# Four places for layer 0's modulation weights, VectorE's rows planned from step 2 on, and tiles of h at multiples of 64 bytes

## The chip, the cores and the metric

One NeuronCore of one Trainium2 chip runs the whole kernel. The metric is the device time of one execution in microseconds. The kernel before was run three times and once more with the hardware profiler; the profile is of that last execution.

## The reference

A network of four layers at width d = 2048 on 256 rows of x and 256 rows of a context. Layer 0 and layer 3 are Fourier layers, layer 1 is windowed attention, layer 2 a convolution layer. Each layer is of this form:

```
shift, scale, gate = split(silu(c) @ ada_w[l])   # "modulation": one column vector per 2048 features
h = rmsnorm(x) * (1 + scale) + shift             # for layer 0 for the context's rows too
z, u = halves of h @ w_in[l]
y = mixing of u with z                           # Fourier, attention or convolution, silu gates
x = x + gate * (y @ w_out[l])
```

Everything is fp32, and the results have to hold fp32's accuracy. The weights alone are over 400 MB read once from device memory.

## The kernel before

Every matrix product of fp32 values is made of three matmuls on split operands: a weight piece `raw` (512 KB or 256 KB) is loaded, ScalarE casts it to `whi` (line 180), VectorE takes `wlo = raw - whi` (line 181), and TensorE adds whi·hh, whi·hl and wlo·hh (lines 193 to 195). hh and hl are the high and low part of a tile of h (lines 457, 458, and 483 for the deferred form); one tile `hx` holds both.

A scheduler sets the order of every engine's instructions from the program's order, data dependences and priorities; `tc.high_priority(offset=...)` raises a block's priority. All weight loads go out on SyncE's queue (SP), in that order, and a load waits there for its place (a buffer of a pool's tag) to be free.

**Layer 0.** h is built while it is used: z = h @ w_in runs in nine `steps` over the 16 k-tiles (two of one k-tile, then seven of two), each step over four column groups (`cg`) of 512 columns, with eight results `accz`. Ahead of step j's h stand step j's modulation columns: `ada_tiles(k, n, j, ...)` computes them in four quarters q of 512 rows each. A quarter loads `aw` (lines 227 to 230, two DMAs) and issues four matmuls into four column groups of one bank `pa` (line 234); after the last, line 240 copies the bank out and line 242 brings it to columns with small matmuls against `sel`. The steps call the generator's next quarter between column groups. Quarters 0 and 1 of each step, and 2 and 3 of steps past the first, have their `aw` tiles in two places of a step's pool; the first step's quarters 2 and 3 lie in `wp`'s four places of tag "aw".

**Rows of later layers.** Beside the steps, `ada_v` computes modulation rows of layer 1 on (loads L330 into wp's "aw", VectorE multiply-adds L281 and L283), and `ada_a` the same on TensorE (L270, L234's kind of matmul). `plan(tiles, calls)` spreads k-tiles over the coming `step()` calls. Before, ada_v's calls start with step JZ = 8, the last; ada_a's also in the last, over four calls.

**colT** is the transposed collection of small parameter vectors: `rt` (L129) is one matmul behind four small loads on ScalarE's queue.

**out_proj** (layers 1 to 3, L1106, L1107) accumulates y @ w_out in banks `acco`; L1117 adds a bank times the gate to xT in two halves and so frees the bank; L418 collects the sum of squares for the next layer's norm, and L437 makes the row sums of it. Layer 3's first part uses a deferred norm (`Deferred`): h is built without the norm's factor (L483), with the shift as two more columns (256, 257) of the tile, and `leave` multiplies by the factor afterwards.

```
JZ = 8
ada_v.plan(TZ, max(1, 4 * (last + 1 - JZ) - 4))
ada_a.plan(A0Z, 4)
```

Of the kernel before, what the change touches and what calls it, by code (L numbers as in the profile page):

```python
# [11 lines left out]
F32 = mybir.dt.float32  # L12
F32R = mybir.dt.float32r
# [28 lines left out]
OWN = 1  # L42
BS = 3
BS3 = 0
JZ = 8
A0Z = 2
PB1 = 0
PB1O = 0
# [22 lines left out]
def dit_kernel(ctx: ExitStack, tc: tile.TileContext, x, c, ctxt, c_ctx, norm_g, ada_w, ada_b,  # L71
# [41 lines left out]
    csil0 = cp.tile([P, 4, 32], F32, name="csil0")  # L113
    nc.gpsimd.memset(csil0[:], 0.0)
    adabT = cp.tile([P, 192], F32, name="adabT")
    ngT = cp.tile([P, 64], F32, name="ngT")
    colT = cp.tile([P, 64], F32, name="colT")
# [63 lines left out]
                eng.tensor_sub(lv[:, c], iv[:, c], hv[:, c].bitcast(F32))  # L181
        return hi, lo

    def gemm_T(outs, piece, rhs, kts, pump=None, span=(0, KT), n=2):

        for i, kt in enumerate(kts):
            whi, wlo = piece(kt)
            for ci, (o, first) in enumerate(outs):
                for k in range(n):
                    hh, hl = rhs(kt + k)  # L190
                    a, b = whi[:, k, ci * P:(ci + 1) * P], wlo[:, k, ci * P:(ci + 1) * P]
                    st = first and kt + k == span[0]
                    mm(o, a, hh, start=st, stop=False, skip_group_check=True)  # L193
# [26 lines left out]
    def ada_tiles(k, n, j, pl, pa):  # L220

        w = 2 * P * n
        for q in range(4):
            if j == 0 and q > 1:
                aw = wp.tile([P, D // 2], F32, tag="aw", bufs=AWB, name=nm("aw"))[:].rearrange("p (k c) -> p k c", k=4)
            else:
                aw = pl.tile([P, 4, 512], F32, tag="aw", bufs=2, name=nm("aw"))
            for i in range(2):
                c0 = (1 - i) * D + P * k
                nc.sync.dma_start(aw[:, :, i * P * n:(i + 1) * P * n],  # L230
                                  ada_w[0, q * 512:(q + 1) * 512, c0:c0 + P * n].rearrange("(k p) c -> p k c", p=P))
            for g in range(4):
                cs = csil[:, 4 * q + g, :] if q else csil0[:, g, :]
                mm(pa[32 * g:32 * g + cs.shape[-1], :w], cs, aw[:, g, :w],  # L234
                   start=q == 0, stop=q == 3, skip_group_check=True)
            if q < 3:
                yield
        with tc.high_priority(offset=FH if j < FJ else 0):
            a = tmp()
            nc.scalar.copy(a[:, :w], pa[:, :w])  # L240
            for i in range(2 * n):
                mm(pa[:, 2 * i:2 * i + 2], a[:, i * P:(i + 1) * P], sel[:], start=True, stop=True)
            for i, c0 in enumerate((16 + k, k)):
                dst = modc[0][:, c0:c0 + n, :]
                nc.vector.tensor_add(dst, pa[:, 2 * n * i:2 * n * (i + 1)].rearrange("p (k o) -> p k o", o=2),
                                     adabT[:, c0:c0 + n].unsqueeze(2).to_broadcast([P, n, 2]))
                if i == 0:
                    nc.vector.scalar_tensor_tensor(dst, dst, 1.0, ngT[:, k:k + n].unsqueeze(2).to_broadcast([P, n, 2]),
                                                   op0=ALU.add, op1=ALU.mult)
        yield  # L250

    def ada_group(l, s, st):
# [209 lines left out]
    WX = 258  # L462

    def new_hx(kt, w=256):
        hx[kt] = hxp.tile([P, 2, w], F32R, tag=f"hx{kt}", name=nm("hx"))
        return hx[kt][:, 0, 0:256], hx[kt][:, 1, 0:256]

    class Deferred:

# [10 lines left out]
        def start(self, kt):  # L480
            hh, hl = new_hx(kt, WX)
            nc.scalar.activation(hh, xT[kt][:], AF.Identity, scale=scale(self.l, kt, 0))
            nc.vector.scalar_tensor_tensor(hl, xT[kt][:], scale(self.l, kt, 0), hh.bitcast(F32),  # L483
                                           op0=ALU.mult, op1=ALU.subtract)
            nc.scalar.copy(hx[kt][:, :, 256:WX], self.sh[:, kt, :].unsqueeze(2).to_broadcast([P, 2, WX - 256]))

        def rhs(self, kt):
            return hx[kt][:, 0, :], hx[kt][:, 1, :]

        def norm(self, st):  # L490

# [15 lines left out]

        def build(self, n):
            for kt in range(self.done, min(KT, self.done + n)):
                build_h(xT[kt][:], self.rs[:], self.l, kt, 0, hx[kt][:, 0, 0:256], hx[kt][:, 1, 0:256])  # L510
# [147 lines left out]
    hp = pool(l0, "h0")  # L658
    stp = ExitStack()
    aw0 = pool(stp, "aw0")  # L660
    psD = pool(l0, "psD0", PSUM)
    psa_box[0] = pool(l0, "psada0", PSUM)
    psA = pool(l0, "psA0", PSUM)
# [101 lines left out]
                     final_g.rearrange("(k p) -> k p", p=P)])  # L765
    h_start(1)
    last = len(steps) - 1
    ada_v.plan(TZ, max(1, 4 * (last + 1 - JZ) - 4))
    ada_a.plan(A0Z, 4)
    for j, (k0, n) in enumerate(steps):  # L770
        if j == 0:
            continue
# [1 line left out]
        for cg in range(4):  # L774
# [113 lines left out]

    def lhs1(kt, m):
        if m < 2:  # L890
            return hx[kt][:, 0, m * P:(m + 1) * P], hx[kt][:, 1, m * P:(m + 1) * P]
# [168 lines left out]
    yh = [None] * 8  # L1060

    def rhsx(kt):
        return hx[kt][:, 0, 0:256], hx[kt][:, 1, 0:256]

    for g in range(4):
        accs = [accA("accz") for _ in range(2)]
# [18 lines left out]
    def out_proj(l, piece, rhs, pmp, after, nxt=None):  # L1085
# [7 lines left out]
        for g, q in order:  # L1093
# [19 lines left out]
            if q == 3:  # L1113
                for ci, o in enumerate(banks.pop(g)):
                    kt = 2 * g + ci
                    for h in range(2):
                        nc.vector.scalar_tensor_tensor(xT[kt][:], o[:, 256 * h:256 * h + 256], gate(l, kt, 0), xT[kt][:],  # L1117
                                                       op0=ALU.mult, op1=ALU.add)
# [19 lines left out]
    def first_chunk(dfr, st, banks, piece, pump):  # L1138
# [10 lines left out]
            elif i > NORM[1]:  # L1149
                dfr.build(2)  # L1150

        gemm_T([(b[:, 0:WX], True) for b in banks], piece, dfr.rhs, range(0, KT, 2), pm)

    ada_v.until(1, 2)
    ada_v.plan(T1O, SV1)
# [163 lines left out]
    for cg in range(4):  # L1319
# [115 lines left out]
```

## Time and profile before

| | |
|---|---|
| median of 3 runs | 1928.76 us (1928.31 to 1929.91) |
| the profiled execution | 1928.43 us, of which its span is 1926.6 |
| TensorE busy | 1859.7 us (97%) |
| VectorE, ScalarE busy | 1447.1 us (75%), 901.2 us (47%) |
| moved by DMA | 433.64 MB, 225 GB/s |

A row of the stretches gives, for a part of the span, how long each engine was busy. The chain that ended last lists, for a time, which instruction or which load the rest waited for. "PE pa L234 <- DMA aw" reads: TensorE's matmul of line 234 waited for the load of a tile aw. A number such as 12.1 behind such a line is microseconds in all, the next the times, the last the longest. In a chain row the count (x8) includes weight loads.

### The profile page before, as it was taken

The page shows a single profiled execution, that of the slowest core. Times are in us where ns is not written, and L with a number is a line of the kernel's source. Part 1 is how long each engine was busy: PE and PEld are TensorE (multiplying, and loading weights), DVE is VectorE, ACT ScalarE, POOL GpSimd, SP SyncE. Part 2 cuts the span into 40 slices and gives each one's busy share as a digit, 9 for nine tenths or more (in the row PEclk, how much of TensorE's full clock was granted, in tenths as well). Part 3 has the DMA queues.
Part 4 walks back from the last instruction along what each step waited for, and adds up shares of the span by engine and source line. Part 5 has one row for each costly group of instructions (what it writes and reads, how often), then busy time and mean ns, then how long its engine had stood idle before and what let it go on. Part 6 is the DMA issues. An engine that isn't in the chain of part 4 may idle for free.

```text
span 1926.6 us, 30182 instructions
## 1 busy us (share of the span) xinstructions
PE 1859.7 (97%) x11143; PEld 1498.1 (78%) x11143; DVE 1447.1 (75%) x2733; ACT 901.2 (47%) x1642; POOL 234.3 (12%) x128
## 2 busy tenths in 40 slices
PE   6999999999999999999999999899999899999997
PEld 5566657777776687866689987899998788888886
DVE  4799954566653458987898696678899999997675
ACT  6333342233321225455556445444455657656553
POOL 0000000000000000000000002688893000000000
PEclk9999999999999999999999999999999999999999
DMA  8888877666677754741567696467776697785553
GB/s 258 273 299 290 304 248 262 204 225 220 237 244 265 263 193 146 242 163 55 186 197 261 205 321 231 148 219 235 230 246 198 212 305 244 246 282 175 164 175 131
DMA packets 247237, 433.64 MB, mean 225 GB/s; under 512 B 16214, under 2 KB 135734, under 8 KB 247090
## 3 DMA queue, kind: packets, MB, share of 16 engines
q1 hardware_dynamic: 245664, 430.00, 67.3%
q10 hardware_dynamic: 1426, 1.73, 0.3%
q8 instruction: 87, 1.43, 0.3%
q14 instruction: 60, 0.49, 0.1%
HBM read 429.56 MB, written 2.10 MB: 224 GB/s over the span
## 4 chain that ended last, share of the span: by engine, by line
PE 77%; DVE 11%; DMA 6%; ACT 3%; issue 3%; SPq 1%; POOL 0%; DVEq 0%; ACTq 0%; POOLq 0%
PE acco L1106 9%; PE accz L193 5%; PE accz L194 5%; PE accz L195 5%; PE acco L1107 4%; PE accu L213 4%; PE accu L215 4%; PE accu L214 4%; DVE wlo L181 3%; DMA aw<-in_ada_w_dram 3%; PE pa L270 3%; PE accg L193 3%; PE accg L195 3%; PE accg L194 3%; DVE pv L1226 3%
## 5 line engine op out<-in xcount | busy, mean ns | idle before, releaser
L180 ACT CAST whi<-raw 128x512 fp32r<-128x512 f32 (+1 forms) x761 | 539.9, 761 | 699.2 <-PE accz L194 135.1
L181 DVE TENSOR_TENSOR wlo<-raw,whi 128x512 fp32r<-128x512 f32 x674 | 491.0, 777 | 211.4 <-ACT whi L180 208.0
L181 POOL TENSOR_TENSOR wlo<-raw,whi 128x1024 fp32r<-128x1024 f32 x87 | 209.7, 2421 | 1230.5 <-ACT whi L180 1227.1
L283 DVE SCALAR_TENSOR_TENSOR adacc<-aw,csil,adacc 128x1024 f32<-128x1024 f32 x188 | 245.5, 1312 | 76.6 <-DMA aw<-in_ada_w_dram 76.2
L1106 PE MATMUL acco<-yh,whi 128*128 128x512 f32 x768 | 272.8, 399 | 3.2 <-DVE xT L1117 3.2
L195 PE MATMUL accz<-hx,wlo 128*128 128x256 f32 (+1 forms) x768 | 218.3, 285 | 5.9 <-DVE wlo L181 5.8
L1107 PE MATMUL acco<-yh,wlo 128*128 128x256 f32 x768 | 216.1, 282 | 3.8 <-DVE wlo L181 3.8
L193 PE MATMUL accz<-hx,whi 128*128 128x256 f32 (+1 forms) x768 | 217.7, 284 | 0.0
L194 PE MATMUL accz<-hx,whi 128*128 128x256 f32 (+1 forms) x768 | 217.2, 283 | 0.0
L1226 DVE SCALAR_TENSOR_TENSOR pv<-gp,dwT,pv 128x256 f32<-128x256 f32 x480 | 191.1, 482 | 20.7 <-ACT pv L1220 20.1
L1106 PEld LDWEIGHTS acco<-yh,whi 128*128 128x128 f32 x768 | 145.4, 190 | 38.3 <-issue 3.8
L195 PEld LDWEIGHTS accz<-hx,wlo 128*128 128x128 f32 x768 | 145.6, 190 | 9.2 <-DVE wlo L181 8.0
L1107 PEld LDWEIGHTS acco<-yh,wlo 128*128 128x128 f32 x768 | 146.0, 190 | 5.6 <-DVE wlo L181 5.4
L195 PE MATMUL accg<-hx,wlo 128*128 128x256 f32 x512 | 145.1, 283 | 2.9 <-POOL wlo L181 2.9
L193 PE MATMUL accg<-hx,whi 128*128 128x256 f32 x512 | 146.1, 286 | 1.1 <-ACT hx L457 1.1
L194 PEld LDWEIGHTS accz<-hx,whi 128*128 128x128 f32 x768 | 146.1, 190 | 1.3 <-issue 0.8
L193 PEld LDWEIGHTS accz<-hx,whi 128*128 128x128 f32 x768 | 146.0, 190 | 1.4 <-issue 0.9
L194 PE MATMUL accg<-hx,whi 128*128 128x256 f32 x512 | 144.6, 283 | 0.0
L193 PE MATMUL acco<-yh,whi 128*128 128x512 f32 (+1 forms) x272 | 106.0, 390 | 0.0
L193 PEld LDWEIGHTS accg<-hx,whi 128*128 128x128 f32 x512 | 97.3, 190 | 8.5 <-issue 6.9
L195 PE MATMUL acco<-yh,wlo 128*128 128x512 f32 (+1 forms) x272 | 103.6, 381 | 0.0
L194 PE MATMUL acco<-yl,whi 128*128 128x512 f32 (+1 forms) x272 | 103.5, 380 | 0.0
(275 smaller groups left out, 3602.2 us busy)
## 6 DMA issues: line engine op xcount, KB each, us to landing
aw<-in_ada_w_dram SPq DMA_DIRECT2D x376, 512.0 KB, 5.5
raw<-in_four_w_in_dram SPq DMA_DIRECT2D x126, 512.0 KB, 4.5
raw<-in_attn_w_in_dram SPq DMA_DIRECT2D x72, 512.0 KB, 3.8
raw<-in_conv_w_in_dram SPq DMA_DIRECT2D x128, 256.0 KB, 2.9
raw<-in_four_w_out_dram SPq DMA_DIRECT2D x32, 512.0 KB, 6.3
raw<-in_attn_w_out_dram SPq DMA_DIRECT2D x64, 256.0 KB, 4.5
raw<-in_conv_w_in_dram SPq DMA_DIRECT2D x32, 512.0 KB, 4.1
raw<-in_conv_w_out_dram SPq DMA_DIRECT2D x64, 256.0 KB, 4.3
```

Source lines behind the costliest of these rows:

```text
L180: nc.scalar.copy(hv[:, c], iv[:, c])
L181: eng.tensor_sub(lv[:, c], iv[:, c], hv[:, c].bitcast(F32))
L193: mm(o, a, hh, start=st, stop=False, skip_group_check=True)
L194: mm(o, a, hl, start=False, stop=False, skip_group_check=True)
L195: mm(o, b, hh, start=False, stop=kt + k == span[1] - 1, skip_group_check=True)
L213: mm(acc[:], hh, whi[:, k, :], start=st, stop=False)
L214: mm(acc[:], hh, wlo[:, k, :], start=False, stop=False)
L215: mm(acc[:], hl, whi[:, k, :], start=False, stop=kt + k == KT - 1)
L283: ins = nc.vector.scalar_tensor_tensor(acc[:, cs], aw[i][:], cc, acc[:, cs], op0=ALU.mult, op1=ALU.add)
L1106: mm(o[:], whi[:, k, cs], rhs(kt), start=kt == 0, stop=False, skip_group_check=True)
L1107: mm(o[:, :256], wlo[:, k, cs], rhs(kt)[:, :256], start=False, stop=kt == KT - 1, skip_group_check=True)
L1226: nc.vector.scalar_tensor_tensor(pv[:, :256], gt[:, t:t + 256], dwT[:, kt, t:t + 1], pv[:, :256], op0=ALU.mult, op1=ALU.add)
```

## The change

It has five parts. Layer 0's quarters 2 and 3 of every step take their tiles from wp's four "aw" places: for a step of two k-tiles each quarter then is two half tiles (two places, four DMAs of 256 KB in place of two of 512 KB), for a step of one k-tile one. ada_v's calls start with step 2 (JZ = 2), 12 k-tiles over 26 calls; ada_a (JA = 8) runs in the last step over two calls. hx becomes a plain tile of 512 or 528 columns with hl at byte 1024 or 1088 (before, the deferred form's hl lay at 1032); the shift's low column stands beside its high one in hh alone, the hl matmul takes 256 columns (`narrow`), and `leave` adds the second column with one small instruction. The residual adds of layers 1 to 3 get priority RES = 200. csil0 moves to the pool of layer 0's start, so layer 1's rows make padded copies of silu(c) for their first four k-tiles too.

```
+JZ = 2
+JA = 8
+RES = 200
...
-                    mm(o, a, hl, start=False, stop=False, skip_group_check=True)
+                    mm(o[:, :narrow] if narrow else o, a, hl, start=False, stop=False, skip_group_check=True)
...
-            if j == 0 and q > 1:
-                aw = wp.tile([P, D // 2], F32, tag="aw", bufs=AWB, name=nm("aw"))[:].rearrange("p (k c) -> p k c", k=4)
+            if q > 1:
+                aws = [wp.tile([P, D // 2], F32, tag="aw", bufs=AWB, name=nm("aw"))[:]
+                       .rearrange("p (k c) -> p k c", k=4 // n) for _ in range(n)]
             else:
-                aw = pl.tile([P, 4, 512], F32, tag="aw", bufs=2, name=nm("aw"))
-            for i in range(2):
-                c0 = (1 - i) * D + P * k
-                nc.sync.dma_start(...)
+                aws = [pl.tile([P, 4, 512], F32, tag="aw", bufs=2, name=nm("aw"))[:]]
+            r = 4 // len(aws)
+            for h, aw in enumerate(aws):
+                for i in range(2):
+                    c0 = (1 - i) * D + P * k
+                    r0 = q * 512 + h * r * P
+                    nc.sync.dma_start(aw[:, :, i * P * n:(i + 1) * P * n],
+                                      ada_w[0, r0:r0 + r * P, c0:c0 + P * n].rearrange("(k p) c -> p k c", p=P))
...
-                if fp and kt < 4:
-                    cs = csil0[:, kt, :]
-                elif fp:
+                if fp:
...
-        hx[kt] = hxp.tile([P, 2, w], F32R, tag=f"hx{kt}", name=nm("hx"))
-        return hx[kt][:, 0, 0:256], hx[kt][:, 1, 0:256]
+        t = hxp.tile([P, 528 if w == WX else 512], F32R, tag=f"hx{kt}", name=nm("hx"))
+        hx[kt] = t[:, 0:w], t[:, 272:528] if w == WX else t[:, 256:512]
...
             nc.scalar.copy(col, bank[:, 256:257])
+            nc.vector.tensor_add(col, col, bank[:, 257:258])
...
-    ada_v.plan(TZ, max(1, 4 * (last + 1 - JZ) - 4))
-    ada_a.plan(A0Z, 4)
+    ada_v.plan(TZ, 4 * (last + 1 - JZ) - 2)
+    ada_a.plan(A0Z, 4 * (last + 1 - JA) - 2)
...
-            if j == last:
+            if j >= JA:
                 ada_a.step()
...
-                    for h in range(2):
-                        nc.vector.scalar_tensor_tensor(xT[kt][:], o[:, 256 * h:256 * h + 256], gate(l, kt, 0), xT[kt][:],
+                    with tc.high_priority(offset=RES):
+                        for h in range(2):
+                            nc.vector.scalar_tensor_tensor(xT[kt][:], o[:, 256 * h:256 * h + 256], gate(l, kt, 0),
...
+        gemm_T([(b[:, 0:WX], True) for b in banks], piece, dfr.rhs, range(0, KT, 2), pm, narrow=256)
```

The scheduler sets the order anew. Three places follow. A tile's number counts the tiles made up to it: aw_382 and aw_421 are step 1's quarters 0 and 1, aw_531 and aw_570 its quarters 2 and 3, aw_617 and the next ones step 2's; aw_2094 and aw_2096 are halves of a row of layer 1.

SP's queue behind the context's loads, before:

```order
L230 DMA aw_382<-in_ada_w_dram 128x4x128 x2
L230 DMA aw_421<-in_ada_w_dram 128x4x128 x2
L156 DMA raw_628<-in_four_w_in_dram 128x512
L156 DMA raw_661<-in_four_w_in_dram 128x512
L230 DMA aw_531<-in_ada_w_dram 128x4x128 x2
L230 DMA aw_570<-in_ada_w_dram 128x4x128 x2
L330 DMA aw_2094<-in_ada_w_dram 128x1024
L230 DMA aw_617<-in_ada_w_dram 128x4x256 x2
L230 DMA aw_650<-in_ada_w_dram 128x4x256 x2
L156 DMA raw_694<-in_four_w_in_dram 128x512
L330 DMA aw_2096<-in_ada_w_dram 128x1024
```

and now:

```order
L235 DMA aw_382<-in_ada_w_dram 128x4x128 x2
L235 DMA aw_421<-in_ada_w_dram 128x4x128 x2
L235 DMA aw_531<-in_ada_w_dram 128x4x128 x2
L235 DMA aw_570<-in_ada_w_dram 128x4x128 x2
L235 DMA aw_617<-in_ada_w_dram 128x4x256 x2
L156 DMA raw_628<-in_four_w_in_dram 128x512
L235 DMA aw_650<-in_ada_w_dram 128x4x256 x2
L156 DMA raw_661<-in_four_w_in_dram 128x512
L235 DMA aw_683<-in_ada_w_dram 128x2x256 x2
L235 DMA aw_684<-in_ada_w_dram 128x2x256 x2
L156 DMA raw_697<-in_four_w_in_dram 128x512
```

Step 1's quarters 2 and 3 moved ahead of the raw weights, and the half rows of layer 1 are gone from here.

TensorE in step 8, the last of layer 0's z, where pa_2171 (now pa_2207) is layer 1's modulation bank and accz the results of z, before:

```order
L195 MATMUL accz_2195<-hh_351,wlo_2199 128x512
L270 MATMUL pa_2171<-aw_2228,csil 2x512 x2
L270 MATMUL pa_2171<-aw_2230,csil 2x512 x2
L270 MATMUL pa_2171<-aw_2236,csil 2x512 x2
L270 MATMUL pa_2171<-aw_2238,csil 2x512 x2
L193 MATMUL accz_2252<-hh_349,whi_2258 128x512
```

and now:

```order
L195 MATMUL accz_2248<-hl_350,whi_2253 128x512
L273 MATMUL pa_2207<-aw_2223,csil 2x512 x2
L196 MATMUL accz_2248<-hh_351,wlo_2254 128x512
L194 MATMUL accz_2249<-hh_349,whi_2253 128x512
L195 MATMUL accz_2249<-hl_350,whi_2253 128x512
L273 MATMUL pa_2207<-aw_2225,csil 2x512 x2
L196 MATMUL accz_2249<-hh_349,wlo_2254 128x512
```

Two groups of four that stood in a row are now pairs between z's matmuls.

VectorE in layer 2's out_proj, at the first residual adds; xT_88 and xT_89 became xT_86 and xT_87 by the count of tiles. Before:

```order
L283 SCALAR_TENSOR_TENSOR adacc_15025<-aw_15322,csil,adacc_15025 128x1024
L1117 SCALAR_TENSOR_TENSOR xT_88<-acco_14967,modc_86,xT_88 128x256
L181 TENSOR_TENSOR wlo_15245<-raw_15241,whi_15244 128x512 x2
L181 TENSOR_TENSOR wlo_15276<-raw_15272,whi_15275 128x512 x2
L1117 SCALAR_TENSOR_TENSOR xT_88<-acco_14967,modc_86,xT_88 128x256
L1117 SCALAR_TENSOR_TENSOR xT_89<-acco_14968,modc_86,xT_89 128x256
```

and now:

```order
L286 SCALAR_TENSOR_TENSOR adacc_15079<-aw_15376,csil,adacc_15079 128x1024
L1125 SCALAR_TENSOR_TENSOR xT_86<-acco_15021,modc_84,xT_86 128x256
L181 TENSOR_TENSOR wlo_15299<-raw_15295,whi_15298 128x512 x2
L181 TENSOR_TENSOR wlo_15330<-raw_15326,whi_15329 128x512 x2
L1125 SCALAR_TENSOR_TENSOR xT_87<-acco_15022,modc_84,xT_87 128x256
L1125 SCALAR_TENSOR_TENSOR xT_86<-acco_15021,modc_84,xT_86 128x256
```

The second bank's first add moved ahead of the first bank's second; the four wlo stay where they were.

More of the change, by code (lines that the diff above doesn't have):

```diff
@@ L44 @@
 BS3 = 0
-JZ = 8
+JZ = 2
+JA = 8
 A0Z = 2
@@ L112, in dit_kernel @@
     csil = cp.tile([P, KT, 2], F32, name="csil")
-    csil0 = cp.tile([P, 4, 32], F32, name="csil0")
-    nc.gpsimd.memset(csil0[:], 0.0)
     adabT = cp.tile([P, 192], F32, name="adabT")
@@ L182, in w_piece, with gemm_T @@
         return hi, lo
-    def gemm_T(outs, piece, rhs, kts, pump=None, span=(0, KT), n=2):
+    def gemm_T(outs, piece, rhs, kts, pump=None, span=(0, KT), n=2, narrow=None):
         for i, kt in enumerate(kts):
@@ L223, in ada_tiles @@
         for q in range(4):
-            if j == 0 and q > 1:
-                aw = wp.tile([P, D // 2], F32, tag="aw", bufs=AWB, name=nm("aw"))[:].rearrange("p (k c) -> p k c", k=4)
-            else:
-                aw = pl.tile([P, 4, 512], F32, tag="aw", bufs=2, name=nm("aw"))
-            for i in range(2):
-                c0 = (1 - i) * D + P * k
-                nc.sync.dma_start(aw[:, :, i * P * n:(i + 1) * P * n],
-                                  ada_w[0, q * 512:(q + 1) * 512, c0:c0 + P * n].rearrange("(k p) c -> p k c", p=P))
+            if q > 1:
+                aws = [wp.tile([P, D // 2], F32, tag="aw", bufs=AWB, name=nm("aw"))[:]
+                       .rearrange("p (k c) -> p k c", k=4 // n) for _ in range(n)]
+            else:
+                aws = [pl.tile([P, 4, 512], F32, tag="aw", bufs=2, name=nm("aw"))[:]]
[6 more added lines that the diff above has]
+                                      ada_w[0, r0:r0 + r * P, c0:c0 + P * n].rearrange("(k p) c -> p k c", p=P))
             for g in range(4):
                 cs = csil[:, 4 * q + g, :] if q else csil0[:, g, :]
-                mm(pa[32 * g:32 * g + cs.shape[-1], :w], cs, aw[:, g, :w],
+                mm(pa[32 * g:32 * g + cs.shape[-1], :w], cs, aws[g // r][:, g % r, :w],
                    start=q == 0, stop=q == 3, skip_group_check=True)
@@ L484, in start @@
                                            op0=ALU.mult, op1=ALU.subtract)
-            nc.scalar.copy(hx[kt][:, :, 256:WX], self.sh[:, kt, :].unsqueeze(2).to_broadcast([P, 2, WX - 256]))
+            nc.scalar.copy(hx[kt][0][:, 256:WX], self.sh[:, kt, :])
         def rhs(self, kt):
-            return hx[kt][:, 0, :], hx[kt][:, 1, :]
+            return hx[kt]
         def norm(self, st):
@@ L509, in build @@
             for kt in range(self.done, min(KT, self.done + n)):
-                build_h(xT[kt][:], self.rs[:], self.l, kt, 0, hx[kt][:, 0, 0:256], hx[kt][:, 1, 0:256])
+                build_h(xT[kt][:], self.rs[:], self.l, kt, 0, hx[kt][0][:, 0:256], hx[kt][1][:, 0:256])
             self.done = min(KT, self.done + n)
@@ L660, in dit_kernel @@
     aw0 = pool(stp, "aw0")
+    csil0 = aw0.tile([P, 4, 32], F32, name="csil0")
+    nc.gpsimd.memset(csil0[:], 0.0)
     psD = pool(l0, "psD0", PSUM)
@@ L890, in lhs1 @@
         if m < 2:
-            return hx[kt][:, 0, m * P:(m + 1) * P], hx[kt][:, 1, m * P:(m + 1) * P]
+            return hx[kt][0][:, m * P:(m + 1) * P], hx[kt][1][:, m * P:(m + 1) * P]
         t = hc[kt // 2]
@@ L1062, in rhsx @@
     def rhsx(kt):
-        return hx[kt][:, 0, 0:256], hx[kt][:, 1, 0:256]
+        return hx[kt][0][:, 0:256], hx[kt][1][:, 0:256]
     for g in range(4):
@@ L1115, in out_proj @@
                     kt = 2 * g + ci
-                    for h in range(2):
-                        nc.vector.scalar_tensor_tensor(xT[kt][:], o[:, 256 * h:256 * h + 256], gate(l, kt, 0), xT[kt][:],
-                                                       op0=ALU.mult, op1=ALU.add)
+                    with tc.high_priority(offset=RES):
+                        for h in range(2):
+                            nc.vector.scalar_tensor_tensor(xT[kt][:], o[:, 256 * h:256 * h + 256], gate(l, kt, 0),
+                                                           xT[kt][:], op0=ALU.mult, op1=ALU.add)
                     if dfr:
@@ L1150, in pm @@
                 dfr.build(2)
-        gemm_T([(b[:, 0:WX], True) for b in banks], piece, dfr.rhs, range(0, KT, 2), pm)
+        gemm_T([(b[:, 0:WX], True) for b in banks], piece, dfr.rhs, range(0, KT, 2), pm, narrow=256)
     ada_v.until(1, 2)
@@ L1335, in dit_kernel @@
         gemm_N(accs, lambda kt: w_piece(w_rows(wi, kt, cg * 512)),
-               lambda kt, m: (hx[kt][:, 0, m * P:(m + 1) * P], hx[kt][:, 1, m * P:(m + 1) * P]),
+               lambda kt, m: (hx[kt][0][:, m * P:(m + 1) * P], hx[kt][1][:, m * P:(m + 1) * P]),
                range(0, KT, 2), pump5u if cg == 0 else ada_v.step)
```

1 line of the change is left out of this document (added).

## The prediction

> **What bounds the kernel now.** I read the page's first block, then the busy time of each engine by stretches, then the chain that ended last where TensorE idles. The page's head:
>
> ```profile
> span 1926.6 us, 30182 instructions
> PE 1859.7 (97%) x11143; PEld 1498.1 (78%) x11143; DVE 1447.1 (75%) x2733; ACT 901.2 (47%) x1642; POOL 234.3 (12%) x128
> ```
>
> TensorE (PE) is busy for all but 67 us. The stretches (us; busy time of PE, weight loads, VectorE, ScalarE, GpSimd; clock, DMA share, GB/s) tell where those lie:
>
> ```profile
> 0.00:80.00 80.00, 60.73 (x363) 40.78 (x363) 44.00 (x96) 43.32 (x87) 0.85 (x7) 0.96 0.82 259
> 80.00:240.00 160.00, 158.19 (x768) 106.66 (x768) 147.66 (x217) 60.35 (x72) 0.00 (x0) 1.00 0.87 297
> 240.00:280.00 40.00, 39.12 (x176) 22.25 (x174) 25.92 (x40) 21.30 (x33) 0.00 (x0) 1.00 0.67 230
> 1440.00:1560.00 120.00, 110.19 (x750) 101.04 (x749) 111.65 (x230) 70.91 (x151) 23.71 (x10) 0.97 0.68 222
> 1560.00:1720.00 160.00, 152.28 (x920) 132.42 (x919) 152.63 (x236) 100.59 (x168) 0.00 (x0) 0.98 0.81 269
> ```
>
> So 19 us can be won in the first 80 us; in layer 0's z steps (80 to 240) only 1.8; in layer 2's out_proj and the way into layer 3 some 17. Everywhere else an added matmul costs its time. The chain at the start (start, length, what), the stretch 30 to 35, SP's issues, and a small load of ScalarE's queue (KB, us to landing):
>
> ```profile
> 36.99 0.38 PE pxt L700 x2
> 37.47 4.26 DMA aw<-in_ada_w_dram
> 41.86 0.66 PE pa L234 x8
> 42.95 9.30 DMA aw<-in_ada_w_dram
> 52.38 1.02 PE pa L234 x2
> 53.60 0.66 PE accz L193 x2
> ```
>
> ```profile
> 30.00:35.00 5.00, 5.00 (x45) 4.67 (x44) 0.69 (x1) 4.72 (x12) 0.00 (x0) 0.91 0.03 10
> ```
>
> ```profile
> 21.24 2.56 SPq L230 DMA_DIRECT2D aw<-in_ada_w_dram  x4
> 35.38 2.59 SPq L230 DMA_DIRECT2D aw<-in_ada_w_dram  x4
> 38.02 0.50 SPq L330 DMA_DIRECT2D aw<-in_ada_w_dram  x1
> ```
>
> ```profile
> tmp<-in_conv_ln_g_dram ACTq DMA_DIRECT2D x1, 8.0 KB, 7.2
> 43.05 0.43 ACTq L126 DMA_DIRECT2D tmp<-in_conv_ln_g_dram  x1
> ```
>
> Step 1's quarters 2 and 3 have no place until PE has used quarters 0 and 1; they are issued at 35.38, after five microseconds in which the DMA engines moved 10 GB/s. All that follows lands late: PE waits to 41.86 and to 52.38, and z of step 1 starts at 53.60.
>
> **The change part by part.**
>
> *Start (A).* In the new order these four loads stand right behind those of 21.24, so they land in the empty stretch, and the half row of layer 1 (38.02) leaves this place: they and it, 1.5 MB by their shapes, no longer stand ahead of step 2's loads. PE then meets its data when its transposes end, at 37.4 in place of 41.86. Step 0's second half (48 matmuls of 128x256; 0.12 us each by the pair rows at the end of this part, 5.8 us) ends near 45. Between it and step 1 now stand the transposition of colT, which needs the four small loads, and one modulation group of 1 us. With no wait, step 1 starts at 46.0 (7.5 us won); if a small load is issued at 43.05 and takes 7.2 as before, at 50.3 + 1.3 = 51.6 (2.0 won). The small loads now share the queues with less traffic; I take 50.4, nearer the row: −3.1.
>
> The modulation matmuls of two steps (ns min, median, max), the chain in the first steps, and a step in steady state; the last row is the time from issue to landing of 12 loads, min, median, max:
>
> ```profile
> L234 PE MATMUL pa<-aw,csil x64: 591/592/617, 101.7 to 150.8; 128*2 128x512 f32 x48, 128*32 128x512 f32 x16
> 73.19 0.31 DVE hl L458
> 74.75 0.95 PE pa L234 x2
> 80.08 0.96 PE pa L234 x6
> 86.82 0.97 PE pa L234 x8
> 96.70:125.10 28.40, 28.09 (x138) 18.99 (x137) 26.48 (x39) 10.73 (x13) 0.00 (x0) 1.00 0.86 296
> 109.54 0.92 SPq L230 DMA_DIRECT2D aw<-in_ada_w_dram  x2
> 116.27 0.92 SPq L230 DMA_DIRECT2D aw<-in_ada_w_dram  x2
> DMA to landing us min/median/max: 5.0/5.5/6.3
> ```
>
> One modulation group, four matmuls side by side in four column groups, takes 0.97 (x8 counts its weight loads too); the one matmul at 74.75 takes 0.95 and its three others 0.96. So a group that the order cuts in two costs 0.95 more. Step 2's aw_650 was cut and is now whole: −1.0. Step 3's first tiles are pulled ahead of a wait of PE for hl (VectorE, to 73.5; the queue of wlo ahead of it is shorter with an earlier start): −1.0, from the some 2 us idle there (bounds 0 and −2), and the one more cut group of step 3 falls into the rest. Start together: **−5.1** (−10 to −2).
>
> By the Trainium skill (TensorE: Matmul & The Clock Gate, Part 3, the mechanism) matmuls in different column groups overlap, and a set lasts about as long as one of them. The trace has 0.592 for one and 0.97 for a set of four, so it agrees only in that the set is far under four times one. By that rule a cut would cost 0.59: B below would be +3.0 and the time 1929.0; I go by the chain's 0.95.
>
> *Cut groups after the start (B).* By the new order steps 7 and 8 have one cut group more each, and layer 1's modulation block on TensorE, whose eight k-tiles now run over the two first column groups of step 8's plan rather than over four, has 22 group times in place of 19. Rows from there:
>
> ```profile
> 262.13 1.03 PE pa L270 x4
> 277.68 0.97 PE pa L270 x8
> PE pa L270 <- DMA aw<-in_ada_w_dram: 0.5, 2, 0.3
> ```
>
> Half a group costs 1.03, a whole one 0.97: 2 × 0.96 + 3 × 1.03 = **+5.0**, all on PE, which is busy 39.12 of 40 us there. Bounds: +3 if two cuts stand where PE would wait for a load anyway, +5.
>
> *Quarter 3's place (C).* From step 3 on, quarters 2 and 3 share two of the four places while rows of layer 1 hold the others, as I read the allocations; so in steps 3 to 5 quarter 3's four loads are issued only when quarter 2's matmuls are done. Before, each quarter was issued when the quarter two ahead of it was done, so a load had two of the 6.73 us between 109.54 and 116.27. Now it has one less the group: 6.73 − 0.97 = 5.8 us, against 5.5 to land plus 0.92 for the two issues of the first half: 0.6 late, the second half up to 1.5. Halves of 256 KB may land sooner than the 5.0 of whole loads: 0 to 1.5 per step, three steps: 0 to 4.5, I take 0.5 per step, near the first half's row: **+1.5**. SP stands still meanwhile; behind it are the next raw weights, of which three are held, so PE does not see that.
>
> By the Trainium skill (DMA: Bandwidth & Descriptors, Bandwidth) loads should be batched to 1 MiB or more, which speaks against halving quarters 2 and 3. No row here prices a half load of this shape; were halves as slow as whole loads, C would be +4.5 and the sum 3 us more.
>
> *Rows over all steps, JZ (D).* The rows added per step look like 1 MB of load and its VectorE work, in steps where VectorE has 26.48 of 28.40. But the scheduler had already hoisted such rows: by both orders the bytes asked for ahead of each raw tile differ by at most 2 MB up to the first u piece and by none from the third on. Zero for that. Ahead of the first u piece the row halves stand 14 in a run now (7 MB, 24 us at the 296 GB/s above) where four stood between raw tiles: bounds 0 and +3, the slack of three raw tiles covers most: **+0.5**.
>
> *Residual adds in out_proj, RES (E).* Rows of layer 2, chain and waits:
>
> ```profile
> 1530.84 0.41 DVE xT L1117
> 1531.38 0.47 PE acco L1106
> 1531.85 0.12 PE acco L1107
> 1533.15 0.43 PE acco L1106
> 1536.32 0.23 PE acco L1106
> PE acco L1106 <- DVE xT L1117: 3.0, 1, 3.0
> PE pss L437 <- DVE ss L418: 2.9, 1, 2.9
> ```
>
> PE waits 3.0 us for the first residual add's bank, then runs at half pace (0.43 for 0.23) from 1533.15 to 1536.32, another 1.6; the way into layer 3 has 2.9, and the clock of 0.98 in its stretch of 160 us is 3 us of full pace. In the new order the four wlo of 128x512 still stand ahead, and one add of the second bank is put before the first bank's second: the first bank is free 0.41 later, **+0.4**. Bounds: −4.6 (stall and tail gone) and +2 (a longer tail).
>
> *Tiles, narrow matmuls, leave (F).* VectorE rows of 1600 to 1720, the first kind with an aligned tile, the second with the 2064-byte one:
>
> ```profile
> L458 DVE SCALAR_TENSOR_TENSOR hx<-tmp,modc,hx 128x256 fp32r<-128x256 f32 x16 | 6.9, 459 | 0.0
> L483 DVE SCALAR_TENSOR_TENSOR hx<-xT,modc,hx 128x256 fp32r<-128x256 f32 x4 | 1.8, 486 | 0.0
> ```
>
> At most 27 ns × 16 = 0.4 won; four small adds (one column each; estimated at 0.15, a third of the 256-column rows) stand in a stretch that VectorE fills (152.63 of 160): **+0.3** (−0.4 to +1). csil0's move and four more pads, small VectorE work ahead of a load that is awaited: 0.
>
> Sum: −5.1 + 5.0 + 1.5 + 0.5 + 0.4 + 0.3 = +2.6. The profiled execution took 1928.43, 0.33 under the median of the runs and inside their spread: 1931.0.
>
> **The rivals.** A change is told from none beyond 0.2%, 3.9 us.
> 1. *Slower, quarter 3's wait:* it takes 1.5 us in each of three steps or reaches the later steps. Sum 2.6 + 3.0 = 5.6, 1934.0; it decides from 0.95 us per step. For it: 5.5 + 1.84 for four issues against 5.8. Against: half the bytes per load.
> 2. *Slower, the small loads:* step 1's start still waits (start term −2): 5.7, 1934.1. For it: 7.2 us for 8 KB. Against: emptier queues.
> 3. *Faster, RES frees out_proj's banks* and PE stays at pace in both places: 2.6 without E's and F's 0.7, less 9: −7.1, 1921.3. For it: 4.6 us lost at the first and, by wait and clock, 4.4 and more at the second. Against: the wlo rows that stay ahead.
> 4. *Faster, start at 46.0*, with two cuts that stand in waits: 2.6 − 4.4 − 2 = −3.8, 1924.6. For it: the empty stretch of the DMA engines from 30 to 35. Against: colT.
> 5. *Nothing measurable:* cuts cost one lone matmul (0.59) each and start pays for them: 0.6, 1929.0.
>
> **How the numbers follow.** Forecast 0.34, rival 1 0.14, rival 2 0.14, rival 3 0.14, rival 4 0.12, rival 5 0.12. The likeliest's own range is 1927 to 1935; with one in ten left out on each side, 1921 to 1939. Faster 0.26, same 0.46, slower 0.28.
>
> **What would show it.** A: SP's eight modulation loads in a row before 30 us, accz of step 1 near 50. B: more pa groups, PE without new waits from 243 on, and u some 5 us later behind z's first step than now. C: waits of PE pa for aw near 0.5 us in steps 3 to 5, and SP waiting for PE there. E: the 3.0 us wait for xT still in layer 2. The prediction is wrong if the stretch 0 to 80 gives back over 8 us or nothing, or if the two late waits are gone.

## The result, and the profile after

The change makes the kernel slower: 1945.59 us (median of 4 runs, 1942.07 to 1949.18) against 1928.53 for the kernel before (1927.74 to 1929.91), a ratio of 1.0088 (95% interval 1.0074 to 1.0102), some 17 us. 1931.0 with a range of 1921 to 1939 was predicted.

The head of the page, and the stretches in which the two kernels can be compared by the clock of the span (same columns as before):

```profile
span 1947.1 us, 30248 instructions
PE 1871.5 (96%) x11143; PEld 1505.1 (77%) x11143; DVE 1447.6 (74%) x2745; ACT 901.0 (46%) x1642; POOL 234.5 (12%) x128
```

```profile
0.00:80.00 80.00, 64.96 (x384) 43.87 (x385) 46.18 (x98) 45.21 (x88) 0.84 (x7) 0.96 0.87 271
80.00:240.00 160.00, 152.93 (x692) 103.21 (x691) 132.25 (x198) 52.93 (x65) 0.00 (x0) 0.95 0.79 261
240.00:280.00 40.00, 37.70 (x169) 22.42 (x168) 29.91 (x47) 19.20 (x26) 0.00 (x0) 1.00 0.74 244
```

In the first 80 us TensorE is busy 4.2 us more than before. In the next 160 us, where it had idled 1.8 us, it now idles 7.1, the clock that it was granted is 0.95 in place of 1.00, and the DMA engines move less, 261 GB/s for 297. So most of the loss is in z's steps, and neither the DMA engines nor VectorE (132 for 148) are fuller than they were.

The steps can be measured by one instruction that each has once, ScalarE's copy of the next step's modulation bank at the step's end (L240, now L245). The first two rows are of the kernel before (step 2's end and step 7's), the others of the changed kernel (step 2's end to step 7's):

```profile
95.22 0.68 ACT L240 COPY tmp<-pa 128x512 f32<-128x512 f32 x1
237.30 0.65 ACT L240 COPY tmp<-pa 128x512 f32<-128x512 f32 x1
```

```profile
92.37 0.77 ACT L245 COPY tmp<-pa 128x512 f32<-128x512 f32 x1
125.98 0.71 ACT L245 COPY tmp<-pa 128x512 f32<-128x512 f32 x1
157.18 0.69 ACT L245 COPY tmp<-pa 128x512 f32<-128x512 f32 x1
188.83 0.70 ACT L245 COPY tmp<-pa 128x512 f32<-128x512 f32 x1
218.89 0.65 ACT L245 COPY tmp<-pa 128x512 f32<-128x512 f32 x1
248.99 0.64 ACT L245 COPY tmp<-pa 128x512 f32<-128x512 f32 x1
```

Before, five steps took 142.1 us, 28.4 each. Now step 2 ends 2.8 us earlier, but steps 3 to 7 take 33.6, 31.2, 31.7, 30.1 and 30.1, together 14.5 more: step 7 ends 11.7 late. The first row sum of layer 1 (L437, now L440) comes at 741.4 in place of 725.4, 16.0 late, so step 8 and u add 4.3.

What a long step waits for is in the chain of waits. The end of step 3:

```profile
115.57 1.19 DVE adacc L286
116.78 0.37 SPq L235
117.19 0.46 SPq L235
117.71 6.40 DMA raw<-in_four_w_in_dram
...
125.09 1.17 ACT whi L180
126.27 0.43 ACT tmp L245
126.74 1.17 PE pa L247 x8
127.92 0.64 PE accz L195
128.55 0.43 PE accz L196
...
131.34 0.23 PE accz L194
```

VectorE finishes with a half row of layer 1 (adacc); that frees its place, which a quarter's load (L235) has waited for at the head of SyncE's queue; only behind it can the next raw weights be issued, which land 6.4 us later. ScalarE casts them, and its copy of the bank stands behind the casts. TensorE stops for 2.2 us, and then its matmuls come every 0.43 us and not every 0.23 until 131. Step 4 ends by the same chain (a half row of VectorE until 148.7, then raw weights that land 5.6 us after their issue at 149.7). The waits of SyncE's queue from 60 to 250, first of the changed kernel, then of the kernel before (us in all, times, longest):

```profile
SPq L235 <- DVE adacc L286: 32.2, 9, 8.5
SPq L333 <- DVE adacc L286: 23.0, 5, 10.9
SPq L235 <- DVE adacc L284: 5.4, 2, 2.8
```

```profile
SPq L230 <- PE pa L234: 86.5, 24, 5.2
SPq L330 <- DVE adacc L283: 3.3, 2, 2.0
```

SyncE stood 3.3 us for VectorE's rows before and stands 60.6 now. The total is not what hurts: all waits that the profile lists for SyncE in these 190 us add up to 137 us before and 131 now. Before, the 86.5 us for a quarter's place left the raw weights in time.

### The profile page after: what moved, and what is told of

Read it like the earlier page. It is cut to its first block, busy times and chain, and to the rows that moved or that the text cites. A ratio compares the mean times of both kernels' runs of the same rounds, so it can differ in the third digit from the quotient of the medians.

```text
span 1947.1 us, 30248 instructions
## 1 busy us (share of the span) xinstructions
PE 1871.5 (96%) x11143; PEld 1505.1 (77%) x11143; DVE 1447.6 (74%) x2745; ACT 901.0 (46%) x1642; POOL 234.5 (12%) x128
## 4 chain that ended last, share of the span: by engine, by line
PE 77%; DVE 10%; DMA 8%; ACT 3%; issue 2%; SPq 0%; DVEq 0%; ACTq 0%
PE acco L1113 7%; PE accz L194 6%; PE accz L195 6%; PE accz L196 6%; PE accu L214 4%; DVE wlo L181 4%; PE accu L216 4%; PE accu L215 4%; PE acco L1114 3%; PE pa L273 3%; DMA aw<-in_ada_w_dram 3%; PE accg L194 3%; PE accg L196 3%; PE accg L195 3%; PE acco L194 3%; PE acco L195 3%
## 5 line engine op out<-in xcount | busy, mean ns | idle before, releaser
L194 PE MATMUL accz<-hx,whi 128*128 128x256 f32 (+1 forms) x768 | 218.0, 284 | 0.0
L195 PE MATMUL accz<-hx,whi 128*128 128x256 f32 x768 | 217.5, 283 | 0.0
L1234 DVE SCALAR_TENSOR_TENSOR pv<-gp,dwT,pv 128x256 f32<-128x256 f32 x480 | 191.1, 483 | 23.4 <-ACT pv L1228 20.5
L795 DVE TENSOR_TENSOR y<-accz,y 128x512 f32<-128x512 f32 x128 | 84.5, 687 | 30.8 <-PE accz L196 30.4
```

Of the source, the lines that this page charges most:

```text
L195: mm(o[:, :narrow] if narrow else o, a, hl, start=False, stop=False, skip_group_check=True)
L795: nc.vector.tensor_add(y, accs[ci][:], y)
L1234: nc.vector.scalar_tensor_tensor(pv[:, :256], gt[:, t:t + 256], dwT[:, kt, t:t + 1], pv[:, :256], op0=ALU.mult, op1=ALU.add)
```

## The experiments

Theory P at first: rows and quarters share places, so loads on SyncE's queue wait for VectorE. Its rivals: quarter 3's own missing place; 256 KB loads; the rows' work itself; the parts behind layer 0. The table has the ends of steps 2 and 7, the step times between, the first row sum of layer 1 (all from one profiled execution each), and the median and ratio of the runs.

| kernel | step 2 ends | steps 3 to 7 | step 7 ends | layer 1 | median, ratio to before |
|---|---|---|---|---|---|
| before | 95.2 | 28.5 28.4 28.3 28.4 28.4 | 237.3 | 725.4 | 1928.5 |
| changed | 92.4 | 33.6 31.2 31.7 30.1 30.1 | 249.0 | 741.4 | 1945.6, 1.0088 |
| rows_late | 92.6 | 28.5 28.4 28.5 28.4 28.5 | 234.8 | 758.0 | 1958.5, 1.0164 (1.0126 to 1.0202) |
| places_alone | 90.9 | 28.4 28.5 28.4 28.4 28.4 | 233.1 | 753.3 | 1959.9, 1.0163 (1.0141 to 1.0185) |
| rows_own_places | 95.2 | 30.2 30.2 30.1 28.4 28.5 | 242.6 | 729.7 | 1935.5, 1.0046 (1.0033 to 1.0058) |
| late_parts_alone | 94.0 | 28.5 28.4 28.5 28.4 28.5 | 236.2 | 724.6 | 1928.6, 1.0005 (0.9990 to 1.0020) |
| rows_on_gpsimd | 90.6 | 29.4 29.1 29.2 29.0 31.4 | 238.6 | 730.8 | 1932.8, 1.0025 (1.0012 to 1.0038) |
| rows_and_quarters_on_gpsimd | 91.9 | 29.1 29.1 29.3 29.0 30.1 | 238.6 | 730.2 | 1936.3, 1.0039 (1.0025 to 1.0052) |
| split_places | 93.9 | 28.8 28.5 29.1 28.4 31.1 | 239.7 | 734.8 | 1945.3, 1.0092 (1.0072 to 1.0111) |
| ada_a_old_plan | 92.0 | 32.3 33.1 30.0 30.1 30.2 | 247.7 | 735.7 | 1942.5, 1.0076 (1.0054 to 1.0098) |
| start_alone | 93.7 | 28.4 28.5 28.3 28.4 28.4 | 235.7 | 723.1 | 1926.2, 0.9993 (0.9981 to 1.0005) |
| places_to_step_3 | 92.4 | 28.5 29.4 28.3 28.4 28.4 | 235.4 | 722.1 | 1925.1, 0.9987 (0.9977 to 0.9997) |

What follows layer 1's start took between 1198.4 and 1208.2 us in these executions (before 1201.2, changed 1205.7); rows_own_places, which has the order of before there row for row, took 1205.9. So of the profiled execution's 20.5 us over before, the last 4.5 are within what one execution differs from another, and the mark at layer 1 is the better measure. The marks have their own spread: ada_a_old_plan has the changed kernel's order of instructions up to 265 us, and its steps 3 to 7 add up to 155.7 us where the changed kernel's have 156.6, with up to 2 us between single steps; rows_late and places_alone have one order up to 280 us, and their step 2 ends at 92.6 and 90.9.

**rows_late**

```
 # the changed kernel
-JZ = 2
+JZ = 8
-    ada_v.plan(TZ, 4 * (last + 1 - JZ) - 2)
+    ada_v.plan(TZ, max(1, 4 * (last + 1 - JZ) - 4))
```

> The changed kernel with ada_v's rows planned as before (JZ = 8, old formula); everything else of the change stays. Theory P (shared places: a modulation load waits on SP for VectorE to finish with a row that holds the place, and the raw weights queued behind it come too late): without rows in steps 2 to 7 no load waits for VectorE, the steps are back at 28.4 us in place of 30.1 to 33.6, and of the 15 us lost in steps 4 to 8 nearly all are won back; 1926 to 1932 in all. Rival Q (quarter 3 has one place less and PE waits for it): the places of quarters 2 and 3 are then free of rows, so four places serve both; this rival gives the same here, 1926 to 1932. Rival H (halves of 256 KB are slower to load): no change, 1940 to 1949. Rival L (the loss lies in the parts behind layer 0): no change.

**places_alone**

```
 # the kernel before, with the changed kernel's loads of quarters:
-            if j == 0 and q > 1:
-                aw = wp.tile([P, D // 2], F32, tag="aw", bufs=AWB, ...)
+            if q > 1:
+                aws = [wp.tile([P, D // 2], F32, tag="aw", bufs=AWB, ...) for _ in range(n)]
```

> The kernel before with the four places alone (ada_tiles of the change, the rows planned as before). Theory P: no rows hold the places during steps 2 to 7, steps at 28.4 us, the start earlier by 2.5 us: 1924 to 1930. Rival H: 256 KB halves are slow, 1940 and over. Rival Q: at most 1935.

Both have steps of 28.4 us, as theory P and rival Q had it, and both are far slower than the changed kernel, which no theory had (rival H's time for places_alone, 1940 and over, came, but not by slower steps). The steps first: with four places and no rows, quarter 3's own wait costs nothing, nor do halves of 256 KB, though SyncE waits long for it. Rivals Q and H fall. A rival that was not named falls as well, that TensorE's new order costs the time: up to 180 us the traces of places_alone and of the changed kernel have TensorE's and ScalarE's instructions in the same order, with steps of 28.4 in the one and of 31.2 to 33.6 in the other. What differs is VectorE's rows and SyncE's loads. PE's waits (60 to 330) and SyncE's (60 to 300) in places_alone, and its last step (step 8, to u's start):

```profile
PE accz L193 <- DVE y L792: 16.9, 4, 9.1
```

```profile
SPq L234 <- PE pa L238: 58.1, 17, 4.7
```

```profile
233.10:291.90 58.80, 39.84 (x146) 25.87 (x145) 51.53 (x64) 21.19 (x32) 0.00 (x0) 0.85 0.85 295
```

Step 8 takes 58.8 us; it was 41.3 before (237.3 to u's first matmul at 278.6). The kernel before has its rows in the program only from step 8 on too, but there the scheduler pulled them into the earlier steps, since wp's places were free; with the quarters in those places it cannot: the kernel before has issued 28 loads of half rows by 237 us, places_alone 6, the first at 225.7. So VectorE has 51.5 us of work in the last step (27.5 before), and PE waits for it to empty its banks (y). That is what the new plan of the rows repairs (step 8 takes 48.7 us in the changed kernel): it is the other half of the change, and without it the places cost 31 us. Step 8 has 17.5 of the 32.1 us that places_alone loses between step 7's end and layer 1; the rest comes in u and was not followed.

**rows_own_places**

```
 # the kernel before
-JZ = 8
+JZ = 2
-    ada_v.plan(TZ, max(1, 4 * (last + 1 - JZ) - 4))
+    ada_v.plan(TZ, 4 * (last + 1 - JZ) - 2)
```

> The kernel before with the rows' new plan alone (JZ = 2, 12 k-tiles over 26 calls): quarters keep their own two places, rows keep theirs. Theory P: rows and quarters share nothing, so SP waits for VectorE only with a row, as before; steps at 28.4 to 28.8 us, 1926 to 1932 in all. A rival W (it is the rows' work itself: 26.5 us of VectorE in a step of 28.4, or their loads): steps at 30 us and more, 1940 or over.

Three steps of 30.2, then 28.4. The time, 1935.5, lies between the two forecasts. It is no rival W: VectorE has 26.5 us in the slow steps as in the quick ones. The three slow steps are the three whose modulation group the order cuts in two, one each; the steps with four whole groups take 28.4. So this run prices a cut, with what comes with it: 1.7 to 1.8 us. TensorE's rows around one:

```profile
103.25 0.40 PE L195 MATMUL accz<-hh,wlo 128*128 128x512 f32 x1
104.06 0.73 PE L193 MATMUL accz<-hh,whi 128*128 128x512 f32 x2 [0.41 <-ACT hh L457]
...
105.42 1.02 PE L234 MATMUL pa<-aw,csil 128*2 128x512 f32 x2
106.37 0.50 PE L194 MATMUL accz<-hl,whi 128*128 128x512 f32 x1
106.70 0.39 PE L195 MATMUL accz<-hh,wlo 128*128 128x512 f32 x1
106.94 0.39 PE L194 MATMUL accz<-hl,whi 128*128 128x512 f32 x1
```

The one matmul holds TensorE from 105.42 to 106.37, the matmul after it takes 0.33 in place of 0.23, likewise the one ahead of it, and 0.41 more goes to a wait for hh, since these matmuls start before h is there.

**late_parts_alone**

```
 # the changed kernel, with before's loads of quarters, and
-JZ = 2
+JZ = 8
-    ada_v.plan(TZ, 4 * (last + 1 - JZ) - 2)
-    ada_a.plan(A0Z, 4 * (last + 1 - JA) - 2)
+    ada_v.plan(TZ, max(1, 4 * (last + 1 - JZ) - 4))
+    ada_a.plan(A0Z, 4)
```

> The changed kernel with layer 0's weights, rows and plans as before: what is left is hx's tiles with the narrow matmuls, the residual adds' priority 200, and csil0's move with four more pads. Theory P: within 3 us of before, 1926 to 1932 (the trace of the changed kernel has 1440 to 1720 within 2 us of before). Rival L: 1934 to 1945.

No change that can be measured: the tiles of h at multiples of 64 bytes, the narrow matmuls, the residual adds' priority and csil0's move together bring at most 2 us and cost at most 4, by the interval. Rival L falls.

Theory P had its place right but not its whole: it became theory T, in which SyncE's queue is what hurts, and cut groups a second cost.

**rows_on_gpsimd and rows_and_quarters_on_gpsimd**

```
 # the changed kernel
+    rowq = [nc.gpsimd]            # back to nc.sync behind z
...
-                nc.sync.dma_start(t[:], ada_w[l, ...])
+                rowq[0].dma_start(t[:], ada_w[l, ...])
 # and in the second of the two
-                    nc.sync.dma_start(aw[:, :, ...
+                    (nc.gpsimd if j > 1 and q > 1 else nc.sync).dma_start(aw[:, :, ...
```

> The changed kernel with the loads of layer 1's rows issued from GpSimd's queue instead of SyncE's while z of layer 0 runs; VectorE's and TensorE's work is the same, as are the places. Theory T (in steps 3 to 5 SyncE stands still before a load whose place a VectorE row still holds, so that the raw weights behind it are issued too late; a cut modulation group costs 1.2 to 1.8 us): only the quarters' own waits for such a place are left on SyncE's queue; the steps that had 33.6, 31.2 and 31.7 us fall to 28.4 to 30.5; step 6 and 7, whose cut groups are gone in this order, to 28.4; 1930 to 1940. Rival B (the places themselves: a quarter's data come late whatever the queue): steps of 31 to 34 us remain, 1942 to 1949.

> As the last one, and quarters 2 and 3 of the steps from the third on are issued from GpSimd's queue too, so SyncE's queue in z's steps holds only raw weights and quarters 0 and 1. Theory T: nothing on SyncE's queue waits for VectorE's rows; every step from 2 to 7 at 28.4 us except where PE waits for a quarter itself; step 7's copy near 233 to 240; layer 1's rows have 23 group times in place of 19, 5 to 7 us; 1926 to 1934. Rival B: steps of 31 to 34 us remain, 1942 to 1949.

With the same places and the same work on VectorE, and another queue for the rows' loads as the only edit (the scheduler set the order anew with it), steps 3 to 5 fall from 33.6, 31.2 and 31.7 to 29.4, 29.1 and 29.2, and the ratio falls from 1.0088 to 1.0025, some 12 us of 17. That is theory T; rival B falls. The quarters' loads still wait on SyncE for VectorE's rows:

```profile
SPq L235 <- DVE adacc L286: 26.6, 12, 4.3
SPq L235 <- DVE adacc L284: 2.3, 2, 2.0
```

28.9 us in all with a longest of 4.3 leave the raw weights in time, where 60.6 with a longest of 10.9 did not; TensorE's granted clock is 1.00 in all of steps 3 to 7. To move the quarters off SyncE as well, where theory T wanted 28.4 in every step, brought no more: 29.0 to 30.1, and 1936.3. What holds these steps at 29 was not settled; the longer step 7 in both neither. About half is to be seen in rows_on_gpsimd's trace: in the new order TensorE waits once a step for hh, which it did not in the kernel before, 2.8 us of the 6.0 that its steps 3 to 7 have over before's:

```profile
PE accz L194 <- ACT hh L461: 2.8, 5, 1.2
```

**split_places**

```
 # the changed kernel: quarters 2 and 3
-... tag="aw", bufs=AWB
+... tag="aq", bufs=2
 # rows; zs is True until z has ended
-... tag="aw", bufs=AWB
+... tag="aq" if h and not zs[0] else "aw", bufs=2
```

> The changed kernel with wp's four places split while z of layer 0 runs: two for layer 1's rows alone, two for quarters 2 and 3 alone (after z all four serve the rows again); every load stays on SyncE's queue. Theory T, in its narrow form (a quarter's load stands in SyncE's queue until VectorE has done with a row in its place): that wait is gone, rows only wait for rows and quarters only for TensorE, which cost nothing in the kernel with the places alone; steps 3 to 5 at 28.4 to 30.5; 1930 to 1938. In its wide form (any load behind VectorE's rows in SyncE's queue, a row's own too, since a row has two places now and not four): SyncE still waits for VectorE, before a row's load, steps 3 to 5 stay at 30.5 to 33; 1938 to 1948.

The steps are those of the narrow form, 28.4 to 29.1 and one of 31.1 with a cut group, though a row's own load still waits on SyncE as the wide form says:

```profile
SPq L334 <- DVE adacc L286: 26.2, 9, 7.9
```

So either kind of wait alone is borne, the quarter's in rows_on_gpsimd and the row's here. That it is the two together, a row's load behind a quarter's and a quarter's behind a row's in four places, that makes raw weights late, fits both runs; no run shows it by itself. What z won is lost behind it: step 7 ends 9.3 us earlier than in the changed kernel, layer 1 starts 6.6 earlier, and the median is no better (1945.3, in the wide form's range). By the order the first block has 23 group times in place of 22; the rest of that loss is open.

**ada_a_old_plan**

```
 # the changed kernel
-    ada_a.plan(A0Z, 4 * (last + 1 - JA) - 2)
+    ada_a.plan(A0Z, 4)
```

> The changed kernel with ada_a's calls in step 8 planned as before (four calls in place of two); the order has 20 group times in layer 1's first modulation block on TensorE in place of 22. Theory T: z's steps as in the changed kernel (33.6, 31.2, 31.7, 30.1, 30.1), and layer 1 starts 2.4 to 3.6 us sooner after step 7 than in the changed kernel (492.4 us from step 7's copy to the first row sum); 1939 to 1946. Rival D (the load of 7 MB of rows ahead of the first piece of u sets this, not the cuts): the same distance as in the changed kernel within 1 us.

From step 7's end to layer 1 it takes 488.0 us, 4.4 less than the changed kernel's 492.4, about before's 488.1. The other kernels agree: with four calls and rows ahead of step 8 this distance is 486.7 to 488.4 us (before, rows_own_places, late_parts_alone, start_alone, places_to_step_3), with two calls 491.7 to 495.1 (changed, both on GpSimd, split_places). So the 4.3 us that step 8 and u add come with the two calls in place of four; two group times fewer, at 1.2 to 1.8 each, would be most of it. PE's waits for loads of rows and for u's first piece hardly differ, 2.7 us here and 3.0 in the changed kernel. Rival D would have left it. The medians, 1942.5 and 1945.6, have overlapping intervals.

**start_alone and places_to_step_3**

```
 # start_alone: the kernel before
-            if j == 0 and q > 1:
+            if j < 2 and q > 1:
 # places_to_step_3: the kernel before, with the changed kernel's loads of quarters and
-            if q > 1:
+            if q > 1 and j < 4:
```

> The kernel before with four places for step 1 alone: its quarters 2 and 3 lie in wp's places, as step 0's do, and are loaded before the raw weights; from step 2 on all is as before. Theory T: the start's gain stands alone: step 2's copy of the modulation bank 2.5 to 3 us earlier than 65.5, step 3's 3 to 4 us earlier than 95.2, steps at 28.4; 1924 to 1926, faster by 0.1 to 0.25%. Rival G (the gain at the start is eaten by a later wait, for a layer or for the rows): within 1 us of before.

> The kernel before with the four places for steps 0 to 3 only (two halves per quarter in steps 2 and 3), the rows planned as before, so that the scheduler's hoisted rows use the places from step 4 on. Theory T: the start's gain of places_alone (step 3's copy at 90.9 in place of 95.2), steps at 28.4 after it, step 8 as before if the rows still come early; 1923 to 1926. Rival G: rows that have less time for being hoisted pile up in step 8, 1928 to 1935.

start_alone has step 2's end 1.5 us earlier and keeps that, but the ratio's interval includes no change. places_to_step_3 is faster than both kernels: 0.9987 (0.9977 to 0.9997), some 2.5 us; step 2 ends 2.8 us earlier, step 7 1.9, layer 1 starts 3.3 earlier. The first row is loaded at 87.6, when the last of these quarters have been loaded, 28 half rows by 237 us as in the kernel before, and they do not pile up.

## Why the prediction was wrong

*The step that failed* is in part C: "SP stands still meanwhile; behind it are the next raw weights, of which three are held, so PE does not see that", and with it part D's "Zero for that". I looked for what happens to a quarter's data and found 0 to 1.5 us per step; PE never waits for a quarter's data from 90 to 250 in the changed kernel, and places_alone prices quarter 3's missing place at nothing. What counts is what else stands in the queue. The order showed rows and quarters alternating in four places, so that a quarter's load waits for VectorE's work on a half row, and a row's load for a quarter's matmuls; I used that for the places alone and did not add up what SyncE's queue would wait for. It stands 60.6 us of 190 for VectorE's rows, the raw weights behind land late, and steps 3 to 5 pay 11.2 us, step 2 some 1.1 (below). Rival 1 had the steps and the direction right, but by a wait of PE for quarter 3's data that did not come, and at a price of 4.5 in all.

*The price of a late transfer* was missing too. The stretch of step 3, then step 7 of the same kernel, which has a cut group but no late weights:

```profile
92.40:126.00 33.60, 31.32 (x136) 21.51 (x136) 26.46 (x40) 10.73 (x15) 0.00 (x0) 0.90 0.74 245
218.90:249.00 30.10, 29.25 (x138) 19.09 (x136) 27.01 (x41) 10.39 (x15) 0.00 (x0) 1.00 0.70 219
```

Of the 5.2 us that step 3 has over the prediction's steady step (28.40, of which 28.09 busy), 2.0 are TensorE's idle time and 3.2 busy time at a lower pace: the tail costs more than the wait. In steps 3 to 5 together it is 3.6 idle and 7.6 busy; step 5 is long by the tail of the wait at step 4's end, at a granted clock of 0.89. By the Trainium skill (TensorE: Matmul & The Clock Gate, Part 1) the clock falls after an idle window of about 3.4 us. Here it fell sooner; the measurement decides: z's last matmul ends near 91.6, and the granted clock is half from 93.4 on. The waits at the ends of steps 2 and 3, each ahead of the small matmuls that turn the bank to columns, what came behind the first of them (chain), and the stretches around it:

```profile
93.19 1.70 PE L247 MATMUL pa<-sel,tmp 128*128 128x2 f32 x8 [1.56 <-ACT tmp L245]
126.74 1.17 PE L247 MATMUL pa<-sel,tmp 128*128 128x2 f32 x8 [2.23 <-ACT tmp L245]
```

```profile
95.53 0.43 PE accz L196
...
99.79 0.43 PE accz L194
100.22 0.29 PE accz L195
100.74 0.23 PE accz L194
```

```profile
89.00:93.40 4.40, 2.84 (x17) 1.10 (x15) 2.38 (x3) 2.58 (x3) 0.00 (x0) 1.00 1.04 379
93.40:100.20 6.80, 6.80 (x21) 5.64 (x21) 6.14 (x15) 1.82 (x4) 0.00 (x0) 0.50 1.08 368
```

A wait of this length does not always have a tail. In split_places, with other matmuls behind it, one of 1.71 us had none (granted clock 1.00 from 232 to 246):

```profile
237.17 1.03 PE L239 MATMUL pa<-aw,csil 128*2 128x512 f32 x4 [1.71 <-DMA aw<-in_ada_w_dram]
```

What decides between the two was not tested.

*Start (A)* was predicted at −5.1 and is −2.8 by the copies at step 2's end. The mechanism is half as said. Ten loads of quarters stand in a row in SyncE's queue, the wait for step 1's quarter at 52.38 is gone, and step 1's z starts 2.6 us earlier, 51.02 for the 50.4 taken. But the way to 50.4 was another: step 0 was to end near 45 and z then to wait for the small loads behind colT. TensorE's matmuls of step 0 run until 49.7, and colT's matmul rt follows without a wait. That the two times are so near is luck.

```profile
21.09 16.03 SPq L235 DMA_DIRECT2D aw<-in_ada_w_dram  x10
```

```profile
49.54 0.28 PE L766 MATMUL accz<-hh,wlo 128*128 128x256 f32 x1
49.75 0.27 PE L129 MATMUL rt<-ident,tmp 64*128 64x64 f32 x1
```

```profile
50.02 0.99 PE pa L239 x8
51.02 0.43 PE accz L194
```

In five kernels with these places for steps 1 and 2 and without late weights in step 2 (rows_late, places_alone, places_to_step_3 and the two on GpSimd) step 2 ends at 90.6 to 92.6: 2.6 to 4.6 us won, below the −5.1; rows_late and places_alone, of one order so far, differ by 1.7 of this. Step 2 itself takes 28.1 to 28.3 us there and 29.4 in the changed kernel, since the first late raw weights come in step 2 already: those issued at 83.08 land at 90.45, and their cast starts at 90.55. That is 1.1 us, less than the spread between executions.

*Cut groups (B)* were priced at 0.95 to 1.03 each and cost more: 1.7 in each of steps 6 and 7, 1.7 to 1.8 in rows_own_places. With D, B's part in step 8 and u was 3.1 + 0.5; 4.3 was measured. The 0.59 us of the prediction and of rival 5 was a misreading: each of these f32 matmuls leaves two MATMUL records (L234 has 288 for 36 quarters of four), so x8 is four matmuls without their weight loads, 0.592 us is one of a matmul's two records, and one matmul holds TensorE for 0.95. By the Trainium skill's rule weighed there (TensorE: Matmul & The Clock Gate, Part 3, the mechanism) a set lasts about as long as one matmul of it. The trace agrees, 0.97 for the set and 0.95 for one, so that rule gives the row's 0.95 for a cut and not 0.59.

*Residual adds (E) and tiles (F)*, +0.4 and +0.3, are not contradicted: late_parts_alone is at 1.0005, with an interval too wide to show terms of this size. The waits are still there in the changed kernel, the second of them 3.3 us for 3.0 before, as E had it:

```profile
PE pss L440 <- DVE ss L421: 3.6, 1, 3.6
PE acco L1113 <- DVE xT L1125: 3.3, 1, 3.3
```

Rival 3 (the stall goes) fell, rivals 2 and 4 (the small loads hold the start, or the start at 46.0) too, and 5 (nothing measurable). Rival 2's start term, −2, is nevertheless nearer to the −2.8 than the forecast's −5.1.

In the sum: 2.6 was predicted and 16.0 measured at layer 1's mark. Of the 13.4 between, 9.7 are steps 3 to 5, where SyncE issues raw weights late (11.2 for the 1.5 of C), 2.3 the start with step 2 (−2.8 for −5.1, 1.1 of it late weights again), 1.4 the cuts of steps 6 and 7 (3.3 for 1.9, step 8's bank among them) and 0.7 step 8 and u (4.3 for 3.6); E's and F's 0.7, which lie behind the mark, go off.

## What to carry to other kernels

A load that waits for its place holds up every load behind it on its queue, so when two users come to share places, see for each wait in the queue which transfer that TensorE needs soon stands behind it; the sum of the waits alone does not tell (137 us before, 131 now). Another queue for the loads that may wait gave back some 12 of 17 us without changing a place. Where a scheduler pulls work forward into free places, taking those places removes the cover even if nothing else moves: here it cost 31 us, more than the whole change. A wait of some 2 us of a busy TensorE can bring a half-pace tail that costs more than the wait, here 3.2 us in one step and 7.6 in three; price it as a bound.

## What was not expected of the hardware

A set of four modulation matmuls in four column groups holds TensorE for 0.97 us, and one alone for 0.95; with the slower matmuls on both sides and the wait for h that it then meets, cutting such a set costs 1.7 us in a step. Waits of 1.6 and 2.2 us, each with eight small matmuls behind it, were followed by matmuls at 0.43 in place of 0.23 us for some 5 and 3 us; one of 1.7 us with other matmuls behind it was not. The same order of instructions behind layer 1 took 1201.2 us in one execution and 1205.9 in another.
